# Laying the second parts of the normed tokens 448 bytes further on in SBUF, with a smaller scratch for dynamic DMAs

## The chip, the cores and the metric

The kernel is one program on one core of a Trainium2 chip. The metric is the device time of one execution in microseconds (us). Three executions of the kernel before took 2135.42, 2138.87 and 2143.49 us; the median is 2138.87 us.

## What is computed

256 tokens of width 1024 pass through two layers and a third block, all in float32. Cut to the lines that matter here, the reference is:

```python
for layer in range(2):
    x = x + mixer(x)                  # rmsnorm, x_n @ w_in, recurrence or attention, @ w_out
    x = x + peer_ffn(x)               # rmsnorm, query, top-k keys, experts
# peer_ffn, for every token t with its 8 heads and 16 chosen experts each:
#   act = gelu(<x_n[t], expert_down[idx]>);  out += g * act * expert_up[idx]
# block 2: rmsnorm, x_n @ w_in_2, pooling and dilated attention, gates, @ w_out_2, final norm
```

There are 16384 experts in a layer. The kernel does not gather the chosen ones: it multiplies the normed tokens by all of `expert_down`, masks, and multiplies by all of `expert_up`.

## The kernel before, in words

**Three matmuls for a float32 product.** Every large product is computed from parts. A float32 operand is split into a first part (rounded to float32r) and a second part (what the rounding left): `xh` and `xl` of the normed tokens, `wh` and `wl` of a weight tile. `mm3` (L431) adds three matmuls into one PSUM tile: first by first, first by second, second by first. All of them are issued in `mm` (L429), so every row of the trace has that line; they are told apart by the names of the tiles.

```python
def mm3(self, out, L, R, first, last):
    self.mm(out, L[0], R[0], start=first, stop=False)
    self.mm(out, L[0], R[1], start=False, stop=False)
    self.mm(out, L[1], R[0], start=False, stop=last)
```

`L` is the stationary operand, which a weight load (PEld) brings into the array, and `R` the moving one, which streams through it. Two kinds of product occur. In kind T the weights are stationary and the tokens move: the three matmuls are `xh,wh`, `xh,wl`, `xl,wh` of one block of 128 rows, each with 256 columns (the tokens), and the trace shows them as they run, in the order `xh,wh`, `xl,wh`, `xh,wl`. In kind N the tokens are stationary and the weights move (256, 448 or 512 columns). A group of eight such triples (24 matmuls) makes one 128x256 result.

**The tiles.** `xh` and `xl` (L388) are two tiles of 8 x 256 float32 (8192 bytes in each partition), allocated one behind the other in the pool that is opened first, and used by all five stages. `Entry.trans` (L202) and `Entry.second` (L215) fill them at the start of each stage. Split weights lie in the pool `ws` (L385, five slots of 4096 bytes for `wh`, five for `wl`), in the peer stages also in tiles `w` of their own (the query weights); `yh`, `yl`, `bh`, `bl`, `mgh`, `mgl` are the split results of block 2, multiplied by `mm3` in the same way.

**The order of the work.** The stages run one after the other: mixer 0, peer 0, mixer 1, peer 1, block 2. `Stream.run` walks a list of products and splits weights ahead of them; in a peer stage `early(e)` computes one group of 24 matmuls `ps<-x` for each of the 128 expert blocks of a layer (256 groups in all), with float16 matmuls for the masks (`oo`, `ah`) between them, and later the products with `expert_up` (`acc<-wh,W` and `acc<-wl,W`, 512 columns). ACT writes `wh` (L498), DVE `wl` (L493). SP issues the loads of weights; POOL issues a few others through its own queue, whose descriptors lie in a scratch at the start of SBUF (16384 bytes of each partition by default).

Of the kernel before, what the change touches and what calls it, by code (L numbers as in the profile page):

```python
# [8 lines left out]
F32R = mybir.dt.float32r  # L9
# [10 lines left out]
S = 256  # L20
D = 1024
KB = D // 128
# [87 lines left out]
class Lin:  # L110
# [5 lines left out]
    def __init__(self, x, W, nk, cols, cn, kind, cb, late=0, k0=0, acc=None, start=True, stop=True,  # L116
                 need=None, mid=None, of=None, pieces=None):
        self.x, self.W, self.nk, self.cn, self.kind, self.cb, self.late = x, W, nk, cn, kind, cb, late
        self.mid, self.of = mid, of
        self.pieces = pieces or range({"T": cn // 128, "N": 2, "N2": 4}[kind])  # L120
        self.k0, self.acc, self.start, self.stop, self.need = k0, acc, start, stop, need
        self.cols = cols if isinstance(cols, tuple) else (cols, cn, 1, cn)
        self.w, self.keep = [], False
        if of:
            of.keep = True
# [248 lines left out]
class Net:  # L374
    def __init__(self, ctx, tc, A):
        self.tc, self.nc, self.A, self.ctx = tc, tc.nc, A, ctx
        nc = self.nc
        P = lambda name, **k: ctx.enter_context(tc.tile_pool(name=name, **k))
        self.cp = P("consts", bufs=1)
        self.raw = P("raw", bufs=4)  # L380
        self.dram = P("dram", bufs=1, space=DRAM)
        self.n = 0
        cp = self.cp
        self.esm = P("esm", bufs=1)
        self.ws = P("ws", bufs=WS)  # L385
        self.pa = P("pa", bufs=4, space=PSUM)
        self.pb = P("pb", bufs=4, space=PSUM)
        self.xn = [cp.tile([128, KB, S], F32R, name=n) for n in ("xh", "xl")]  # L388
        self.ident = cp.tile([128, 128], F32, name="ident")
        nc.scalar.dma_start(self.ident, A["c_ident"])  # L390
        self.vec = cp.tile([128, NVEC], F32, name="vec")
        self.entry = self.brow = None
# [1523 lines left out]
```

## Time and profile before

| | |
|---|---|
| median of 3 executions | 2138.87 us (2135.42 to 2143.49) |
| the profiled execution | 2143.46 us, of which the span from first to last instruction is 2141.7 us |
| busy share of the span | PE 98%, PEld 90%, DVE 72%, ACT 53%, POOL 9% |
| granted TensorE clock, mean | 0.994 |

The profiled execution is 0.2% above the median. Matmuls are pipelined: the time given for one of them (some 280 ns for 256 columns) is from its start to its modelled end, and the next one starts while it still runs. The pace at which matmuls follow each other is read from the starts: so many matmuls between two start times. A timeline row carries its start with two decimals of a microsecond, so the pace of single matmuls is seen only over many.

### The profile page before, as it was taken

Reading aid. Unit: us, or ns where it says so; the run is one execution under the profiler, and the core shown is the slowest. Engines: PE = TensorE matmul, PEld = TensorE weight load, DVE = VectorE, ACT = ScalarE, POOL = GpSimd, SP = SyncE. Lnnn points to the kernel's source line nnn. Section 1 sums busy time; section 2 is a strip of 40 time slices with the busy share of each in tenths; the row PEclk is TensorE's granted clock in tenths of the full one; section 3 lists DMA queues with packets and bytes.
Section 4 is the critical chain, followed back from the end, with each engine's and each line's share of the span. In section 5 each row is a group of like instructions: output and inputs, shape, how many; then the busy total and the mean of one; then the engine's idle time right before and its main releaser. Section 6 shows DMA issues by size and latency. Waiting matters only on the chain.

```text
span 2141.7 us, 37623 instructions
## 1 busy us (share of the span) xinstructions
PE 2096.7 (98%) x14793; PEld 1924.8 (90%) x14793; DVE 1550.7 (72%) x2904; ACT 1124.7 (53%) x1944; POOL 198.0 (9%) x131
## 2 busy tenths in 40 slices
PE   8999999999999999998999999999999999999998
PEld 7989999999888889987799999998888899899998
DVE  7869978997666665667689789986666667644565
ACT  6345555554455454557456555555555555545443
POOL 2310210000000000012101200000000000122223
PEclk9999999999999999999999999999999999999999
DMA  7663554545666666734454645456666658475443
GB/s 247 235 228 108 180 174 153 164 150 169 195 194 191 194 197 206 251 118 138 139 187 147 198 148 159 152 163 193 193 194 195 199 193 264 154 213 147 144 145 115
DMA packets 165581, 382.19 MB, mean 178 GB/s; under 512 B 13137, under 2 KB 82444, under 8 KB 165148
## 3 DMA queue, kind: packets, MB, share of 16 engines
q1 hardware_dynamic: 160544, 364.95, 54.0%
q0 software_dynamic: 4672, 14.76, 2.0%
q8 instruction: 116, 1.90, 0.4%
q14 instruction: 61, 0.50, 0.1%
q10 hardware_dynamic: 188, 0.09, 0.0%
HBM read 376.56 MB, written 8.43 MB: 180 GB/s over the span
## 4 chain that ended last, share of the span: by engine, by line
PE 88%; DVE 8%; ACT 2%; issue 1%; DMA 1%; SPq 0%; ACTq 0%; DVEq 0%
PE acc L429 53%; PE ps L429 30%; DVE wl L493 2%; ACT wh L498 1%; PE bsc L429 1%; PE bo L429 1%; PE sc L429 0%; PE lev L429 0%; DMA wraw<-in_l_w_in_dram 0%; PE bpt L1776 0%; DVE CI L1229 0%; DVE s L1224 0%; PE ps L208 0%; ACT scr L902 0%; ACT TF L1256 0%
## 5 line engine op out<-in xcount | busy, mean ns | idle before, releaser
L493 DVE TENSOR_TENSOR wl<-raw,wh 128x1024 fp32r<-128x1024 f32 x484 | 600.1, 1250 | 134.0 <-ACT wh L498 133.2
L429 PE MATMUL acc<-wh,W 128*128 128x512 f32 x1984 | 619.6, 389 | 0.0
L429 PE MATMUL ps<-xh,wh 128*128 128x256 f32 x2048 | 582.0, 284 | 0.0
L429 PE MATMUL ps<-xh,wl 128*128 128x256 f32 x2048 | 576.0, 281 | 0.0
L429 PE MATMUL ps<-xl,wh 128*128 128x256 f32 x2048 | 575.8, 281 | 0.0
L498 ACT ACTIVATE wh<-raw 128x1024 fp32r<-128x1024 f32 x504 | 526.6, 1053 | 73.7 <-PE ps L429 55.4
L429 PEld LDWEIGHTS acc<-wh,W 128*128 128x128 f32 x1984 | 372.3, 188 | 75.8 <-DVE W L1460 0.4
L429 PEld LDWEIGHTS ps<-xl,wh 128*128 128x128 f32 x2048 | 390.7, 191 | 1.9
L429 PEld LDWEIGHTS ps<-xh,wh 128*128 128x128 f32 x2048 | 388.1, 190 | 2.0
L429 PEld LDWEIGHTS ps<-xh,wl 128*128 128x128 f32 x2048 | 388.6, 190 | 0.1
L429 PE MATMUL acc<-wl,W 128*128 128x512 f32 x992 | 386.0, 389 | 0.0
L429 PEld LDWEIGHTS acc<-wl,W 128*128 128x128 f32 x992 | 186.1, 188 | 36.9 <-DVE wl L493 0.4
L1459 ACT ACTIVATE W<-ZB 128x256 fp32r<-128x256 f32 x168 | 91.3, 543 | 176.6 <-PE acc L429 152.9
L493 DVE TENSOR_TENSOR wl<-wraw,wh 128x1024 fp32r<-128x1024 f32 (+1 forms) x110 | 144.3, 1321 | 47.9 <-ACT wh L498 47.5
L498 ACT ACTIVATE wh<-wraw 128x1024 fp32r<-128x1024 f32 (+1 forms) x140 | 144.4, 1044 | 48.3 <-PE acc L429 35.4
L1460 DVE TENSOR_TENSOR W<-ZB,W 128x256 fp32r<-128x256 f32 x168 | 89.5, 533 | 100.3 <-ACT W L1459 100.3
L429 PE MATMUL acc<-xh,wh 128*128 128x256 f32 x480 | 135.7, 283 | 0.0
L429 PE MATMUL acc<-xl,wh 128*128 128x256 f32 x480 | 132.9, 277 | 0.0
L429 PE MATMUL acc<-xh,wl 128*128 128x256 f32 x480 | 132.8, 277 | 0.0
L189 POOL TENSOR_TENSOR ZB<-X,gain 128x512 f32<-128x512 f32 x4 | 5.2, 1292 | 1276.8 <-ACT ZB L187 1276.8
L1503 ACT ACTIVATE ZB<-acc 128x352 f32<-128x352 f32 (+30 forms) x128 | 47.6, 372 | 123.2 <-PE acc L429 119.3
L429 PE MATMUL acc<-wh,xh 128*128 128x256 f32 (+2 forms) x336 | 106.7, 317 | 0.9 <-ACT scr L902 0.9
(412 smaller groups left out, 3058.8 us busy)
## 6 DMA issues: line engine op xcount, KB each, us to landing
raw<-in_l_down_t_dram SPq DMA_DIRECT2D x256, 512.0 KB, 4.3
raw<-in_l_peer_expert_up_dram SPq DMA_DIRECT2D x248, 512.0 KB, 4.3
wraw<-in_l_w_in_dram SPq DMA_DIRECT2D x36, 512.0 KB, 4.9
wraw<-in_w_in_dram SPq DMA_DIRECT2D x36, 512.0 KB, 3.9
wraw<-in_l_peer_w_query_dram SPq DMA_DIRECT2D x32, 512.0 KB, 5.1
wraw<-in_w_in_dram SPq DMA_DIRECT2D x48, 256.0 KB, 3.4
wraw<-in_l_w_out_dram SPq DMA_DIRECT2D x16, 512.0 KB, 4.4
brow<-row POOLq DMA_DIRECT2D x1, 5120.0 KB, 32.2
```

Of the source, the lines that this page charges most:

```text
L189: nc.gpsimd.tensor_tensor(y, x, self.gB[:, ns], op=OP.mult)
L429: self.nc.tensor.matmul(*a, **k)
L493: (eng or self.nc.vector).tensor_tensor(lo, r, hi.bitcast(F32), op=OP.subtract)
L498: self.nc.scalar.activation(hi, r, AF.Copy)
L1459: nc.scalar.activation(h, act, AF.Copy)
L1460: nc.vector.tensor_tensor(l, act, h.bitcast(F32), op=OP.subtract)
L1503: nc.scalar.activation(ZB[:, f - E0:, t4], pv[:, f:], AF.Copy, scale=1.0 / GSC)
```

## The change

Two edits, and no instruction is added, removed or moved: on every engine the sequence of instructions and the tiles they name are the same, only line numbers behind the first edit are two higher.

```diff
-        self.xn = [cp.tile([128, KB, S], F32R, name=n) for n in ("xh", "xl")]
+
+        self.xn = [cp.tile([128, KB * S + p], F32R, name=n)[:, q:q + KB * S].rearrange("p (k t) -> p k t", k=KB)
+                   for n, p, q in (("xh", 0, 0), ("xl", 128, 112))]
...
-    nc = _bacc.Bacc("TRN2", target_bir_lowering=False, num_devices=1)
+    nc = _bacc.Bacc("TRN2", target_bir_lowering=False, num_devices=1, dynamic_dma_scratch_size=8192)
```

The tile `xl` becomes 512 bytes longer, and the part that is used starts 448 bytes into it. The scratch of POOL's DMA queue at the start of SBUF is halved to 8192 bytes. With the longer tile alone the largest pool of the peer stage would not fit: it needs 88 kb of a partition, and 87.53 kb would be left. Everything behind `xl` therefore lies 7680 bytes lower than before (8192 less, 512 more). The byte addresses within a partition, and what is left of them after dividing by 128:

| tile | before | mod 128 | after | mod 128 |
|---|---|---|---|---|
| `xh` | 16512 | 0 | 8320 | 0 |
| `xl` | 24704 | 0 | 16960 | 64 |
| `wh`, first slot (the others 4096 apart) | 50112 | 64 | 42432 | 64 |
| `wl`, first slot (the others 4096 apart) | 70592 | 64 | 62912 | 64 |
| `w`, first of the query weights | 196672 | 64 | 188992 | 64 |
| `W`, one of two | 137152 | 64 | 129472 | 64 |
| `yh`, `yl` (block 2) | 174144, 178240 | 64 | 166464, 170560 | 64 |
| `bh`, `bl` (block 2) | 157248, 161344 | 64 | 149568, 153664 | 64 |
| `mgh`, `mgl` (block 2) | 124480, 132672 | 64 | 116800, 124992 | 64 |

The slices that one matmul reads are 512, 1024 or 2048 bytes long and start at multiples of 512 bytes within these tiles, so the remainders hold for every matmul.

## Rows read from the trace of the kernel before

**Rows 1.** The page: span, busy time of the engines, clock in 40 slices, last chain.
```profile
span 2141.7 us, 37623 instructions
...
PE 2096.7 (98%) x14793; PEld 1924.8 (90%) x14793; DVE 1550.7 (72%) x2904; ACT 1124.7 (53%) x1944; POOL 198.0 (9%) x131
...
PEclk9999999999999999999999999999999999999999
...
PE 88%; DVE 8%; ACT 2%; issue 1%; DMA 1%; SPq 0%; ACTq 0%; DVEq 0%
```

**Rows 2.** Groups by form: line, engine, tiles, shapes, count, busy us, mean ns, idle.
```profile
L429 PE MATMUL ps<-xl,wh 128*128 128x256 f32 x2048 | 575.8, 281 | 0.0
...
L429 PE MATMUL acc<-xl,wh 128*128 128x256 f32 x480 | 132.9, 277 | 0.0
...
L429 PE MATMUL acc<-wh,xl 128*128 128x256 f32 x256 | 72.2, 282 | 0.0
...
L429 PE MATMUL acc<-xl,w 128*128 128x256 f32 x192 | 53.4, 278 | 0.0
...
L429 PE MATMUL acc<-wh,mgl 128*128 128x256 f32 x64 | 18.1, 283 | 0.2 <-DVE mgl L1660 0.2
```

**Rows 3.** The chain in order of time: start us, length us, what.
```profile
282.69 25.44 PE ps L429 x216
...
1205.39 24.50 PE ps L429 x216
```

**Rows 4.** The tile xl: count, duration ns minimum/median/maximum, first and last start.
```profile
L429 PE MATMUL ps<-xl,wh x2048: 276/281/415, 156.7 to 1844.8; 128*128 128x256 f32 x187
...
L429 PE MATMUL acc<-xl,wh x480: 276/276/286, 26.4 to 2107.5; 128*128 128x256 f32 x160
```

**Rows 5.** Timeline of PE in block 2 (start, length): 192 matmuls lie between the two.
```profile
1898.44 0.28 PE L429 MATMUL acc<-xh,wh 128*128 128x256 f32 x1
...
1920.20 0.28 PE L429 MATMUL acc<-xh,wh 128*128 128x256 f32 x1
```

**Rows 6.** Timeline of PE: the first y and, 96 matmuls on, the first b.
```profile
2071.06 0.28 PE L429 MATMUL acc<-yh,wh 128*128 128x256 f32 x1
...
2082.58 0.28 PE L429 MATMUL acc<-bh,wh 128*128 128x256 f32 x1
```

**Rows 7.** Timeline of PE: a b group of 24 between two groups of x.
```profile
2090.69 0.28 PE L429 MATMUL acc<-xl,wh 128*128 128x256 f32 x1
2090.80 0.28 PE L429 MATMUL acc<-xh,wl 128*128 128x256 f32 x1
2090.91 0.28 PE L429 MATMUL acc<-bh,wh 128*128 128x256 f32 x1
2091.03 0.28 PE L429 MATMUL acc<-bl,wh 128*128 128x256 f32 x1
...
2093.76 0.28 PE L429 MATMUL acc<-xh,wh 128*128 128x256 f32 x1
```

**Rows 8.** Timeline of PE: x groups of 24 right behind y or b, and their ends.
```profile
2085.46 0.28 PE L429 MATMUL acc<-xh,wh 128*128 128x256 f32 x1
...
2088.19 0.28 PE L429 MATMUL acc<-xh,wh 128*128 128x256 f32 x1
...
2102.27 0.28 PE L429 MATMUL acc<-xh,wh 128*128 128x256 f32 x1
...
2105.01 0.28 PE L429 MATMUL acc<-xh,wh 128*128 128x256 f32 x1
```

**Rows 9.** Windows: stretch, length, busy us (count) of each engine, clock, DMA share, GB/s.
```profile
311.00:518.00 207.00, 207.00 (x1960) 203.86 (x1959) 185.45 (x309) 106.41 (x245) 0.00 (x0) 1.00 0.50 155
```

**Rows 10.** DMA queues and POOL's issues: count, KB each, median us to landing.
```profile
q0 software_dynamic: 4672, 14.76, 2.0%
...
brow<-row POOLq DMA_DIRECT2D x1, 5120.0 KB, 32.2
...
skT<-in_l_keys_t_dram POOLq DMA_DIRECT2D x2, 1024.0 KB, 10.2
```

## Prediction
> **What bounds the kernel now.** The page first: PE is busy 98% of the span, the last chain of waits is 88% PE, and the granted clock is at its full level in all 40 slices [rows 1]. So the end is set by how fast matmuls follow each other, and no wait or clock stands between them that an edit could take out. The windows say the same of the stretch that matters most, the expert products: in 207 us PE is busy 207.00 us, and DVE, the next engine, 185.45 us [rows 9]. DVE is near enough to become the bound if PE gained over 10% there, which is not in question here.
>
> The groups by form give the number of triples in kind T, the kind in which the tokens move past stationary weights: 2048 `ps`, 480 `acc` with `wh`, 192 with `w`, 2720 together [rows 2]. Their chain shows what the reader would not expect: the same 216 matmuls, with the same tiles and shapes at the same clock, take 25.44 us in one place and 24.50 us in another [rows 3], or 117.8 and 113.4 ns each. The tile `xl` shows the same two paces as durations: a single matmul of `ps` has a minimum of 276 and a median of 281 ns, of `acc` a median of 276 [rows 4]. The short pace at its cleanest lies in block 2: 192 matmuls in 1920.20 - 1898.44 = 21.76 us, 113.33 ns each, 340.0 ns a triple [rows 5]. The long pace makes 3 x 117.78 = 353.3 ns.
>
> Once in a pace, PE stays there until something interrupts it. I counted the groups of 24 by their starts in the timeline of the whole run: long are 212 of the 256 `ps` groups, 6 of the 59 whole `acc` groups and 16 of the 24 query groups. With 8 triples a group that is (212 + 6 + 16) x 8 = 1872 long triples of 2720, and the excess over an all-short run is 1872 x 13.3 ns = 25.0 us.
>
> A third pace belongs to operands that lie elsewhere. `y` moves at 64 mod 128, as its weights do: 96 matmuls take 2082.58 - 2071.06 = 11.52 us, 120.0 ns each [rows 6]. `b`, also at 64, entered from a short stretch, takes (2093.76 - 2090.91) / 24 = 118.75 ns [rows 7]. I found no group of either at 113.3. In kind N the multiplication by `mgl` at 64, and the product of `xl` at 0, have means of 283 and 282 ns: both already long [rows 2].
>
> **The change part by part.** No instruction is added, removed or moved. Three things differ.
>
> *The scratch of POOL's queue is halved.* That queue carries 4672 packets at 2.0% of the DMA engines' time [rows 10]. Its large issues are few: `brow` lands 32.2 us after issue, `skT` 10.2 us [rows 10], and their readers come far later; POOL is busy 9% [rows 1]. If descriptors had to wait for space, a landing would be late, not a matmul. Bounds: 0, and at most the three landings shown once over, 32.2 + 2 x 10.2 = 52.6 us, if each were read at once. Taken: 0, because PE waits for none of them; the cover that would have to fail is the work between issue and use.
>
> *All other tiles move down by 7680 bytes*, a multiple of 512. Their remainders, and those of `xh`, stay. In the trace the products with `w`, which starts at another multiple than `wh` but at the same remainder, have a mean of 278 ns, between the 276 and 281 of the two paces [rows 2, 4]: the remainder seems to be what matters, so 0.
>
> *`xl` goes from 0 to 64 mod 128.* It is the moving operand of one matmul in three of kind T, and the stationary one of one in three in kind N. What a mixed triple costs (two moving operands at 0, one at 64, weights at 64) no row shows, so I bound it:
> - From below: two matmuls at the short pace and one at the dearer one of `b`, 2 x 113.33 + 118.75 = 345.4 ns. All 2720 triples so: 2720 x 5.4 = 14.7 us above all-short, less the 25.0 now paid: -10.3 us.
> - From above: all three at the pace of `y`, 360.0 ns. 2720 x 20.0 - 25.0 = +29.4 us.
> - Below the lower bound: the mixture also frees the stream from the long pace and costs nothing itself, 340.0 ns: -25.0 us. No row excludes it; it is rival A.
>
> Between them I go by the nearest rows, x groups right behind `y` or `b`. Two such groups of 24 take 2088.19 - 2085.46 = 2.73 and 2105.01 - 2102.27 = 2.74 us [rows 8], against 24 x 113.33 = 2.72. So a disturbance leaves a tail of 10 to 20 ns in the matmuls after it. In the mixed triple only two matmuls at 0 follow before the next at 64; I let about 7 ns of the tail fall into them: 340 + 5.4 + 7 = about 352 ns. All 2720 triples at it: 2720 x 12 ns = 32.6, less 25.0, is +7.6 us. Every triple would then cost about what a long one costs now, and the sum differs mainly by the 848 triples that are short now (848 x 12 = 10.2 us lost, 1872 x 1.3 = 2.4 us won).
>
> In kind N `acc<-wh,xl` (256 triples) is already at 282 [rows 2]; about 3 us of excess lie there (256 x 3 x some 4 ns). It could lose as much again as `mgl` exceeds it (1 ns), or be freed: -3.4 to +1.7 us. Taken: 0.
>
> **Sum.** Scratch 0, other tiles 0, kind T +7.6, kind N 0: +7.6 us on the profiled execution of 2143.46 (span 2141.7). That execution is 0.2% above the median of 2138.87, to which I apply the difference: 2146.5 us. Own range of this case: 345.4 ns less nothing (-10.3) to a triple of 354 (2720 x 14 - 25.0 = +13.1), with kind N's +1: 2128 to 2153.
>
> **Rivals.**
> - **A: the offset keeps PE from falling into the long pace.** For it: the long pace occurs with exactly today's addresses and depends on how two streams, the moving tokens and the weight load, happen to stand to each other, since tiles, shapes and clock are the same in both [rows 3]; putting one of three reads 64 bytes elsewhere could break that lock. Against it: everything at 64 that the trace shows is dear [rows 6, 7]. All T triples short: 2138.9 - 25.0 = 2113.9 us. It decides from the point at which a mixed triple costs under 345 ns.
> - **B: the address has no effect on the pace**, the difference between x and `y` comes from something else, such as the order of stages. Then 2138.9. For it: x itself has a long pace near that of `b` (117.8 and 118.75). Against it: `y` and `b` leave the short pace at the first matmul and x returns to it within one group [rows 7, 8].
> - **C: the mixed triple locks at the pace of `y`.** 360.0 ns, +29.4 us: 2168 us, slower. Its place is the 256 `ps` groups, its price 6.7 ns a matmul; slower than now from 1872 x 13.3 / 2720 = 9.2 ns above a short triple, 349.2 ns. For it: the steady pace of `y` [rows 6] is reached where no matmul at 0 lies between; against it: two of three matmuls here are at 0.
> - **D: the smaller scratch holds POOL back**, up to the 52.6 us above, most likely some 20: 2160. Against it: the queue's 2.0% [rows 10].
>
> On B the Trainium skill has a rule ("TensorE: Matmul & The Clock Gate", Part 2, the step-by-step section): weight loads and moving operand have two independent read ports of SBUF, and loading "doesn't steal SBUF read bandwidth from the running matmul". By that rule the address of `xl` would not matter and the time would stay at 2138.9 us. The trace bears it out only in part: weight loads are busy in the same 207 us as the matmuls (203.86) without opening gaps [rows 9], but 113.3 and 117.8 ns of one shape remain unexplained by it.
>
> **How the numbers follow.** Chances: forecast 0.42, A 0.30, B 0.10, C 0.16, D 0.02. A measurement of this kernel can tell about 0.5% from no change, 10.7 us: 2128.2 to 2149.6. The forecast's case puts about 0.31 inside, 0.10 above and 0.01 below; B lies inside, A below, C and D above. Faster 0.31, same 0.41, slower 0.28. The range must hold A, which alone has 0.30, so it reaches down to 2112 (all short, and some of kind N); C and D, 0.18, may be left out, and the upper end is the forecast's own with its share of tail, 2156. As cases of both signs hold much of the chance, the likeliest one's own range is 2128 to 2153.
>
> **What would show it.** In the profile after: 216 matmuls of `ps` in the chain near 25.3 us (forecast), 24.5 (A), 25.44 in most and 24.50 in some places (B), 25.9 (C). The x groups of block 2, all short now, at 2.82 us instead of 2.72 (forecast), unchanged (A, B). The groups of `y` and `b` unchanged in any case; should they change, the address of something else matters than I think. Landings of POOL's queue as before, or D. The forecast is wrong if mixed triples settle outside 345 to 354 ns, or if they too have two paces.

## The result

The changed kernel takes 2156.99 us (median of 5 executions, 2152.13 to 2158.83) beside 2139.52 us for the kernel before (5 executions). The ratio is 1.0076, with a 95% interval from 1.0064 to 1.0088: slower by 0.76% (the medians lie 17.5 us apart), and the whole interval lies above the 0.5% that a measurement of this kernel can tell from no change. The forecast was +7.6 us. The direction that came, slower by over 0.5%, had been given a chance of 0.28, less than the 0.41 for "same".

### The profile page after: what moved, and what is told of

It reads as the page before. It is cut to its first block, busy times and chain, and to the rows that moved or that the text cites. A ratio compares the mean times of both kernels' runs of the same rounds, so it can differ in the third digit from the quotient of the medians.

```text
span 2157.1 us, 37623 instructions
## 1 busy us (share of the span) xinstructions
PE 2112.7 (98%) x14793; PEld 1938.9 (90%) x14793; DVE 1555.3 (72%) x2904; ACT 1124.6 (52%) x1944; POOL 197.4 (9%) x131
## 4 chain that ended last, share of the span: by engine, by line
PE 87%; DVE 9%; ACT 2%; issue 1%; DMA 0%; DVEq 0%; ACTq 0%
PE acc L431 54%; PE ps L431 28%; DVE wl L495 3%; ACT wh L500 1%; PE bsc L431 1%; PE bo L431 1%; PE lev L431 1%; DVE s L1226 1%; PE sc L431 0%; PE ps L208 0%; PE bpt L1778 0%; DVE eq L1309 0%; DVE CI L1231 0%; DVE eq L1312 0%; DVE eq L1305 0%
```

## The profile after

The page of the changed kernel, to be read against [rows 1]: span, busy time, chain of waits.

```profile
span 2157.1 us, 37623 instructions
...
PE 2112.7 (98%) x14793; PEld 1938.9 (90%) x14793; DVE 1555.3 (72%) x2904; ACT 1124.6 (52%) x1944; POOL 197.4 (9%) x131
...
PEclk9999999999999999999999999999999999999999
...
PE 87%; DVE 9%; ACT 2%; issue 1%; DMA 0%; DVEq 0%; ACTq 0%
```

The span grew by 15.4 us and PE's busy time by 16.0, with the same 14793 matmuls at the same clock. PE idles no more than before: 2157.1 - 2112.7 = 44.4 us against 45.0. So no wait came in; the matmuls themselves follow each other more slowly.

The landmarks of the chain in order of time (start us, length us, engine, tile, number), first in the kernel before:

```profile
509.31 269.48 PE acc L429 x1188
...
1434.26 266.41 PE acc L429 x1174
...
1866.37 56.72 PE acc L429 x462
...
2065.37 42.54 PE acc L429 x360
```

and in the changed one:

```profile
283.68 25.64 PE ps L431 x216
...
511.88 269.50 PE acc L431 x1188
...
1211.99 25.64 PE ps L431 x216
...
1443.49 266.40 PE acc L431 x1174
...
1877.02 57.73 PE acc L431 x462
...
2080.29 42.97 PE acc L431 x360
```

With the first two landmarks before in [rows 3], the shift of each start tells where the time goes: +0.99 us up to the `ps` stretch of peer 0, +1.58 through its experts to 509.31, +0.02 through the 512-column products, +6.60 - 2.59 = +4.0 up to 1205.39 (the rest of peer 0, mixer 1 and the start of peer 1), +2.6 through the experts of peer 1, +1.4 behind them, +4.3 in block 2 up to its tail, +0.5 to the end. The stretches with kind T pay, and the long stretches of 512-column products, which do not touch `xl`, take as long as before (269.50 and 266.40 us). Added up from start to start over both traces, kind T takes 15.6 us more, the 512-column products of the peer stages 1.5 more and kind N 1.0 less.

The pace itself: both `ps` stretches take 25.64 us, 118.7 ns a matmul and 356.1 ns a triple. Where before one took 25.44 and one 24.50 [rows 3], both now show the same pace. It is a mean: by the matmul that starts, the steps in `ps` (from one start to the next) are 119.7 ns (`xh,wh`), 118.8 (`xl,wh`) and 117.8 (`xh,wl`). The durations agree. Tile `xl` (count, then minimum/median/maximum ns):

```profile
L431 PE MATMUL ps<-xl,wh x2048: 277/282/415, 156.9 to 1855.5; 128*128 128x256 f32 x187
...
L431 PE MATMUL acc<-xl,wh x480: 277/283/287, 26.5 to 2122.8; 128*128 128x256 f32 x160
```

Against [rows 4] the median of `acc` went from 276 to 283. In block 2, where before 192 matmuls took 21.76 us [rows 5], the timeline of PE has

```profile
1908.93 0.28 PE L431 MATMUL acc<-xh,wh 128*128 128x256 f32 x1
...
1931.73 0.28 PE L431 MATMUL acc<-xh,wh 128*128 128x256 f32 x1
...
2086.03 0.28 PE L431 MATMUL acc<-yh,wh 128*128 128x256 f32 x1
...
2097.42 0.28 PE L431 MATMUL acc<-bh,wh 128*128 128x256 f32 x1
```

22.80 us for the same 192 (118.75 ns), and 11.39 us for the 96 of `y`, which had 11.52 [rows 6]: `y` is no dearer than `x` now, and a little cheaper than before. POOL's queue is as it was [rows 10]:

```profile
brow<-row POOLq DMA_DIRECT2D x1, 5120.0 KB, 33.0
...
skT<-in_l_keys_t_dram POOLq DMA_DIRECT2D x2, 1024.0 KB, 9.8
```

## The experiments

My theory going in was that an operand at 64 mod 128 is dear wherever the other one stands ("place"). Its rivals: what counts is how the moving operand and the weights loaded beside it stand to each other ("relation"); the scratch or the shift of everything else did it; any distance between the two parts costs. In all runs below the scratch is 8192 bytes, and r is (address of `wh` - address of the moving `xh`) modulo 512 or, once that is found to suffice, 256. The kernel before has r = 320 for both parts; in the changed kernel r is 320 for `xh` and 384 for `xl`. The query weights `w` stand elsewhere: 196672 - 50112 is 128 more than a multiple of 256, so their distance is r + 128 modulo 256.

**The scratch alone.** The changed kernel with the old line for the tiles:

```diff
-                   for n, p, q in (("xh", 0, 0), ("xl", 128, 112))]
+                   for n, p, q in (("xh", 0, 0), ("xl", 0, 0))]
```

> Scratch of 8192 bytes, xl at 0 mod 128 as before; all tiles move down by 8192 bytes. If the place of xl made the loss (my theory): ratio to before 1.000 +- 0.002, most ps stretches of 216 matmuls at 25.44 us and some at 24.50, x groups of block 2 at 2.72 us. If the smaller scratch or the shift of everything else made it: ratio 1.007 to 1.009 and stretches near 25.6 us.

Measured: 2139.41 us against 2139.66, ratio 1.000 (0.999 to 1.0009). Its chain has the short pace in both stretches of this execution:

```profile
283.99 24.50 PE ps L431 x216
...
1202.05 24.50 PE ps L431 x216
```

The scratch and the move of all tiles by a multiple of 512 cost nothing that shows; the place of `xl` is the cause. That the two stretches were long and short before, and short and short here, belongs to the scatter between the two paces: in `ps` 13% (peer 0) and 21% (peer 1) of the neighbouring starts lay at most 114 ns apart before, and 24% and 22% do here.

**Other distances for `xl` alone.** 384 bytes in place of 448 in v2, 256 in v8:

```diff
-                   for n, p, q in (("xh", 0, 0), ("xl", 128, 112))]
+                   for n, p, q in (("xh", 0, 0), ("xl", 128, 96))]
...
+                   for n, p, q in (("xh", 0, 0), ("xl", 128, 64))]
```

> Like the change, but xl starts 384 bytes into its longer tile instead of 448: 0 mod 128, 384 mod 512. If only the remainder mod 128 counts: ratio 1.000 +- 0.002, both paces as before. If any distance from a multiple of 512 between the two parts costs: ratio 1.007 to 1.009, ps stretches of 216 near 25.6 us.

> The change with 256 bytes in place of 448: xl still starts in its longer tile, scratch 8192. If the pace repeats with 256 bytes of distance, xl stands to wh as xh does, and nothing is mixed: ratio 1.000 +- 0.002, both paces, x groups of block 2 at 2.72 us. If any displacement of xl against xh costs: 1.004 to 1.008.

Measured: 384 bytes 2148.11 us, ratio 1.0044 (1.0027 to 1.006); 256 bytes 2139.39 us, ratio 0.9997 (0.9988 to 1.0007). The first fell between both expectations and refuted each: the remainder mod 128 is that of the kernel before, yet it costs over half of what the change costs. Its chain shows the long pace in both stretches,

```profile
282.46 25.45 PE ps L431 x216
...
1203.79 25.44 PE ps L431 x216
```

while 256 bytes, tried after the sweeps below had suggested a period of 256, behaves as no shift at all:

```profile
281.35 24.50 PE ps L431 x216
...
1201.91 24.50 PE ps L431 x216
```

So not every distance between the parts costs, and the remainder that counts is that mod 256.

**Place or relation.** In v3 64 bytes of padding behind the vector of constants bring the weights to 0 mod 128, where `xh` and `xl` stand unshifted; in v5 (second part of the diff, without the first) both `xh` and `xl` go to 64, where the weights stand:

```diff
-        self.vec = cp.tile([128, NVEC], F32, name="vec")
+        self.vec = cp.tile([128, NVEC + 16], F32, name="vec")[:, :NVEC]
...
-                   for n, p, q in (("xh", 0, 0), ("xl", 128, 112))]
+                   for n, p, q in (("xh", 128, 112), ("xl", 128, 112))]
```

> Scratch of 8192 and 64 bytes of padding behind the vector of constants: xh and xl stay at 0 mod 128, and all weights, y, b and mg come to 0 as well. Theory 'relation' (a matmul is dear when its moving operand and the weights loaded beside it have the same remainder): all kind T at the pace of y, 360 ns a triple, against a mean of 351: +20 to +25 us, ratio 1.009 to 1.012, and no 113.3 ns anywhere. Theory 'place' (an operand at 64 is dear wherever the other one is): all triples at 340 ns or less, y and b too, and the 512-column matmuls of expert_up below their 226.7 ns: -25 to -45 us, ratio 0.979 to 0.988. If neither counts: 1.000.

> Both xh and xl at 64 mod 128, weights at 64 as before. Theories 'relation' and 'place' both: every kind-T triple at the pace of y, 356 to 360 ns, +14 to +25 us against before, ratio 1.0065 to 1.012. If the mixture of two remainders in one triple makes the loss, and not the remainder 64 itself: as before or better, 0.99 to 1.000.

Measured: v3 2156.89 us, ratio 1.009 (1.0072 to 1.0108); v5 2158.07 us, ratio 1.0085 (1.0068 to 1.0102). v3 is the run that felled my theory: with every operand at 0 the time should have dropped by 25 us or more, and it rose by 17 us. Both runs have r = 384, and the same pace. v3:

```profile
282.75 25.63 PE ps L431 x216
...
1207.74 25.62 PE ps L431 x216
```

v5:

```profile
284.34 25.62 PE ps L431 x216
...
1211.71 25.63 PE ps L431 x216
```

The relation counts. Its size was overrated: 118.7 ns in the `ps` stretches, not the 120 of `y`. The query products bear the relation out at a second place of the weights: their mean step is 119.8 ns at distance 0 (v3, v5) and 118.7 at 128 (s1 below), close to `ps` at the same distances (119.7 and 118.9).

**The sweep over r.** `xh` and `xl` get longer tiles and an offset for each stage, the stationary `W` of the 512-column products one for each layer, so that one kernel measures several distances:

```diff
+    def xat(self, stage):
+        return [t[:, q:q + KB * S].rearrange("p (k t) -> p k t", k=KB) for t, q in zip(self.xbuf, XOFF[stage])]
...
-            xh, xl = self.xn
+            xh, xl = self.xat(f"p{l}")
...
-                        w2 = T(wk, [128, 2, S], F32R, "W")
+                        w2 = T(wk, [128, 2 * S + 128], F32R, "W")[:, WOFF[parity]:WOFF[parity] + 2 * S].rearrange("p (a t) -> p a t", a=2)
```

> Scratch 8192; xh and xl shifted together, by another amount in each stage, so that the distance r = (address of wh - address of xh) mod 512 is 192 in mixer 0, 0 in peer 0, 256 in mixer 1, 64 in peer 1, 128 in block 2 (320 in all stages before). The distance of the stationary W from the moving wh in the 512-column products is 64 in layer 0 and 128 in layer 1 (0 before). Theory 'relation mod 128' : at r = 0, 128, 256 no short pace, 356 ns a triple; at 64 and 192 both paces as before, 340 and 353; the 512-column matmuls at 64 below their 226.7 ns (by up to 6.7), at 128 unchanged. Then ps of peer 0 near 356, of peer 1 between 340 and 353, block 2 near 356. Theory 'eight places of 64 bytes' (only one or two distances are bad, r = 384 among them): 340 at most of the new distances, and the total below before by up to 20 us.

> As the sweep before it, with r = 448 in mixer 0, 128 in peer 0, 0 in mixer 1, 192 in peer 1, 256 in block 2; W against wh at 192 in layer 0 and 256 in layer 1. Relation mod 128: ps of peer 0 near 356 ns a triple, of peer 1 between 340 and 353, block 2 near 356; the 512-column matmuls below 226.7 ns in layer 0 and unchanged in layer 1. Eight places: 340 at most distances.

> As the sweeps before it, with r = 64 in mixer 0, 256 in peer 0, 192 in mixer 1, 448 in peer 1, 0 in block 2; W against wh at 320 in layer 0 and 384 in layer 1. Relation mod 128: ps of peer 0 near 356 ns a triple, of peer 1 between 340 and 353, block 2 near 356; the 512-column matmuls below 226.7 ns in layer 0 and unchanged in layer 1. Eight places: 340 at most distances.

Measured: 2167.75, 2157.81 and 2173.95 us, ratios 1.0147 (1.0123 to 1.0171), 1.009 (1.0073 to 1.0106) and 1.0168 (1.0151 to 1.0185). The chain of the first sweep, with r = 0 in peer 0 and 64 in peer 1 (`ps`), and W against `wh` at 64 and 128 (the stretches of over 1000):

```profile
281.32 25.91 PE ps L435 x216
...
511.18 277.27 PE acc L435 x1188
...
1215.88 24.50 PE ps L435 x216
...
1444.75 273.08 PE acc L435 x1174
```

the second, r = 128 and 192, W at 192 and 256:

```profile
284.73 25.63 PE ps L435 x216
...
512.74 272.07 PE acc L435 x1188
...
1210.12 25.44 PE ps L435 x216
...
1440.03 266.40 PE acc L435 x1174
```

and the third, r = 256 and 448, W at 320 and 384:

```profile
281.07 25.90 PE ps L435 x216
...
510.92 277.27 PE acc L435 x1188
...
1215.18 25.44 PE ps L435 x216
...
1445.10 274.20 PE acc L435 x1174
```

What repeats with 256 is now plain: 0 and 256 give 25.91 and 25.90, 128 and 384 give 25.63 each, 192 and 448 give 25.44 each. Of these stretches only those at 64 and 320 have the 24.50. The rule of mod 128 was right for 0, 128 and 256 and wrong for 192 and 448: the long pace is there, but hardly a short one (counted in the trace, 2% of the neighbouring starts of `ps` lie at most 114 ns apart, against 33% at r = 64). The query products, which stand at 192 in the kernel before, say otherwise: 34% of their steps are short there. So 192 has both paces too, and r alone does not tell how often the short one occurs. The 512-column products went the other way than expected: 269.48 and 266.41 us at 0 are the best, 64 costs 7.8 us and 128 6.7 (384 in the third sweep 7.8), and the losses of the first sweep are 14.5 of the 28 us by which the first sweep's kernel is slower.

**Between the multiples of 64.** Only the numbers in the two tables of offsets change.

> After the sweeps the pace of kind T repeats with 256 bytes of distance r: 119.7 ns at 0 and 256, both paces (33% of the matmuls short) at 64, 118.8 at 128 and 384, 117.7 and never short at 192 and 448; the 512-column matmuls have 226.7 to 227.3 at 0 and 256 and 229 to 233 elsewhere. Here r is 32 in peer 0, 96 in peer 1, 64 in all of block 2, 192 in mixer 1 (kind N), and 320 in mixer 0; W against wh at 32 in layer 0 and 224 in layer 1. If the reads go in pieces of 64 bytes: r = 32 and 96 behave like one of their neighbours (119.7 or 118.8, or both paces). If the distance counts byte by byte: means between the neighbours, 117 to 119. If some finer distance is free of the loss: 113.3 in a peer stage, 10 us less for that stage. Block 2 at 64 as at 320: near 114.1 ns with 0.8 of the matmuls short.

> As the run before it, with r = 48 in peer 0, 80 in peer 1, 72 in block 2, 64 in mixer 0, 448 in mixer 1; W against wh at 16 in layer 0 and 240 in layer 1. Pieces of 64 bytes: 48 and 80 like one of their neighbours; byte by byte: both near the 116.4 of 64, a little above; a free distance: 113.3. The 512-column matmuls at 16 and 240 near the 226.7 of 0, or below if a small distance frees them (220).

Measured: 2165.15 and 2162.79 us, ratios 1.0129 (1.0112 to 1.0146) and 1.0116 (1.009 to 1.0141). The tail of block 2 is shown too. r = 32 and 96, block 2 at 64:

```profile
282.41 25.55 PE ps L435 x216
...
1213.77 25.35 PE ps L435 x216
...
2086.39 42.54 PE acc L435 x360
```

r = 48 and 80, block 2 at 72:

```profile
284.33 25.75 PE ps L435 x216
...
1208.81 25.76 PE ps L435 x216
...
2081.76 43.17 PE acc L435 x360
```

None of the three ideas holds quite. Over its whole stage 96 lies between its neighbours (118.5 ns), and so does 32 (118.3). But 16 bytes above 64 the short pace is gone (119.3 ns, none of the steps short), and 16 bytes below it 9% of the steps are short, though the stretch of the chain is a long one (119.2 ns). Block 2 at r = 64 keeps its tail of 360 matmuls at 42.54 us, as at 320; at 72 that takes 43.17. Between its `x` matmuls that is 114.1 and 119.9 ns: the short pace exists at r = 64 and is gone 8 bytes above it. The 512-column products took 228.0 and 228.5 ns at 16 and 240, above the 226.7 of 0 and not below, and 233.4 and 233.3 at 32 and 224; at those two distances they make most of the loss of the first of these runs.

In one table: a `ps` stretch of 216 in us and by 216 in ns, then the whole stage, as the mean of the neighbouring `ps` starts up to 135 ns apart and the share of them that is short (at most 114 ns):

| r mod 256 | stretch, us | stretch, ns | stage, ns | short |
|---|---|---|---|---|
| 0 | 25.90, 25.91 | 119.9 | 119.7 | 1% |
| 32 | 25.55 | 118.3 | 118.3 | 0% |
| 48 | 25.75 | 119.2 | 118.6 | 9% |
| 64 | 24.50 or 25.44 | 113.4 or 117.8 | 116.3 to 117.2 | 13 to 33% |
| 80 | 25.76 | 119.3 | 119.3 | 0% |
| 96 | 25.35 | 117.4 | 118.5 | 1% |
| 128 | 25.62, 25.63 | 118.7 | 118.9 | 0% |
| 192 | 25.44 | 117.8 | 117.7, 117.8 | 2% |
| `xh` 64, `xl` 128 (the change) | 25.64 | 118.7 | 118.8 | 4% |
| `xh` 64, `xl` 192 (v2) | 25.44, 25.45 | 117.8 | 117.8 | 2 to 4% |

**A better place.** In v2 kind N of block 2 had become short (113.2 and 114.0 ns between starts, where before it had 117.8), and there the stationary parts, `xh` and `xl`, stood at 192 and 64. So the same was tried for kind T: the second part of the weights 128 bytes further on, the moving parts together. In s6 this holds for `ps`, with `wh` and `wl` at 64 and 192 in peer 0 and, by moving `xh` and `xl` 128 bytes there, at 192 and 64 in peer 1; in s7 they are at 64 and 192 in both, and in the queries too (the last part of the diff, in s7 alone):

```diff
+WLQ = 32
...
-        hi, lo = places or (pool.tile([128, 1024], F32R, name=self.uid(t), tag=t)[:, :n] for t in ("wh", "wl"))
+        if places:
+            hi, lo = places
+        else:
+            hi = pool.tile([128, 1024], F32R, name=self.uid("wh"), tag="wh")[:, :n]
+            lo = pool.tile([128, 1024 + (64 if pool is self.ws else 0)], F32R, name=self.uid("wl"), tag="wl")[:, q:q + n]
...
-                         for x in self.split_weights(self.ws, down_raw.pop(e), eng=eng)]
+                         for x in self.split_weights(self.ws, down_raw.pop(e), eng=eng, q=WLQ)]
...
-                    hl, r = T(wp, [128, 2, 1024], F32R, "w"), units[u]
+                    hl, r = T(wp, [128, 2048 + 64], F32R, "w"), units[u]
+                    hl = [hl[:, 32:1056], hl[:, 1088:2112]]
```

> A search for a better place, from one finding: in the run with xl 384 bytes further (v2), kind N of block 2, whose stationary operands xh and xl stood at r = 192 and 64, ran at 113.2 to 114.0 ns with 0.97 of the matmuls short, while kind T, whose moving operands were mixed in this way, lost its short pace. Here the stationary operands of ps are mixed instead: wl of expert_down lies 128 bytes further than wh (modulo 256), so that wh and wl stand at r = 64 and 192 in peer 0, and at 192 and 64 in peer 1 (there xh and xl are both shifted by 128 bytes); all else as before. If mixing the stationary operand frees the short pace: ps near 340 ns a triple in one or both peer stages, 10 us less for each, down to 2117 to 2121 us, ratio 0.990. If any mixture costs, as in the change: 353 to 356, ratio 1.002 to 1.005.

> xh and xl as before; the second part of the weights at r = 192 and the first at 64, in the ps groups of both peer stages and in the queries (in the run before, peer 0 had it so: 84% of its matmuls short, 114.2 ns; peer 1, the other way round, 51% and 115.9). Scratch 8192. Expected: ps at 114.2 ns in both stages, 1024 triples x 3 x 1.7 = 5 us less than that run, and about 1 us from the queries: 2124 us, ratio 0.992 to 0.994. If peer 1 stays at 115.9: 2130, ratio 0.996.

Measured: s6 2131.19 us, ratio 0.996 (0.9946 to 0.9974); s7 2125.39 us against 2139.85, ratio 0.9938 (0.9924 to 0.9951), faster than both kernels. The chain of s6, peer 0 and peer 1,

```profile
279.61 24.52 PE ps L436 x216
...
1190.98 25.68 PE ps L436 x216
```

of s7,

```profile
280.41 24.54 PE ps L432 x216
...
1190.23 24.52 PE ps L432 x216
```

and its groups by form; the mean of the first of them was 281 ns before [rows 2]:

```profile
L432 PE MATMUL ps<-xl,wh 128*128 128x256 f32 x2048 | 567.6, 277 | 0.0
L432 PE MATMUL ps<-xh,wl 128*128 128x256 f32 x2048 | 567.6, 277 | 1.3 <-DVE wl L496 1.3
```

Counted by neighbouring starts, some 85% of the `ps` steps of s7 are short, where 13% (peer 0) and 21% (peer 1) were before. In s6 peer 0 has 85% and peer 1, with the two distances the other way round, 52% (116.0 ns on average, though the stretch of its chain is a long one). So in `ps` 64 for the first part and 192 for the second is the better order, and the reverse still beats both at 64. In kind N the order 192, 64 held 97% (block 2 of v2); why the order counts in one and not in the other is open.

## Why the prediction came out as it did

**What bounds the kernel** held: PE, its pace, no wait and no clock. The place where the change would act held too: the loss is in kind T, 15.6 us of a growth of 15.4, with small terms of both signs beside it.

**The step that failed in size** is the price of a mixed triple: "I let about 7 ns of the tail fall into them: 340 + 5.4 + 7 = about 352 ns". It costs 356.1 ns. In place of 2720 x 12 ns the term is 2720 x 16.1 = 43.8 us, and less the 25.0 that the long pace already cost the sum is +18.8, not +7.6. The idea behind it, two matmuls at the short pace and one disturbed, is not what happens: all three steps of the triple are long, 117.8 to 119.7 ns, with the mean of a stream that is wholly at r = 128. The bounds of 345.4 and 360.0 held it; the forecast's own range ended at 354. Kind T grew by 15.6 us in the two traces, 3.2 less than 18.8. Of these, 2.4 lie in interruptions of `ps`: starts more than 135 ns apart, 133 of them with 37.8 us before, 103 with 31.9 after; over 118 ns each that is an excess of 22.1 and 19.7 us. Whether the change did this is not shown: v8, at the pace of the kernel before, has 103 with 31.5 us too. Kind N, which I set to 0, gained 1.0 us; in block 2 its steps went from 117.8 to 115.6 ns. Its upper bound of +1.7 us does not follow from the 1 ns given for it (256 x 3 x 1 ns is 0.8 us); only the +1 at the upper end of the forecast's own range rests on it.

**The step that failed in kind** is the reason given for it, "everything at 64 that the trace shows is dear", read as the remainder of one tile mod 128. Neither place, 0 or 64 mod 128, is dear in itself (v3, v5); what counts is the distance between the moving operand and the weights, mod 256. `y`, `b` and `mgl` are dear because they stand at 128 mod 256 from their weights, not because they stand at 64. By its shift `xl` went from 64 to that same distance. The conclusion for `xl` came out right by luck of the addresses: for moving operands the rows had shown 64 mod 128 only in that relation. The query weights, taken as proof that the remainder mod 128 is what matters, stood at 192 where `wh` stands at 64: at the two distances the long paces are alike (117.8 ns), which hid the difference. The other zero, for tiles that move by a multiple of 512, was right (v1).

**The rivals.** A (the offset frees the stream) is refuted for this change, but not foolish: moving another second part, that of the weights, frees most of the stream in s7. Its condition, a mixed triple under 345 ns, was the right one to name. B (no effect) is refuted by v1 beside the change: same scratch, 1.000 against 1.0076. The Trainium skill's rule that was weighed there ("TensorE: Matmul & The Clock Gate", Part 2, step by step: two read ports, and loading weights takes no bandwidth from the running matmul) leaves no room for the distance of the two operands; here, with the same instructions, that distance alone moves the pace from 113.4 to 119.9 ns, and the measurement decides. C (the pace of `y`, 360 ns) came nearer than the forecast did, 3.9 ns off where I was 4.1: about a draw, with the truth between. D is refuted by v1, and by landings that stayed at 33.0 and 9.8 us.

**The chances.** 0.28 for slower, of which C had 0.16 and the forecast's upper tail 0.10, was too little; the 0.30 for A rested on the argument that any displacement might break a lock, and I had no row for it. The outer range, 2112 to 2156, holds 2138.87 x 1.0076 = 2155.1; the median of the changed kernel's own runs is 1 us above it. With a growth of more than twice the forecast, that it came so near the edge and not beyond it is luck. Of the signs named, the chain near 25.3 us came out at 25.64, the `x` groups of block 2 at 24 x 118.75 = 2.85 us instead of 2.82, and "`y` and `b` unchanged" was wrong for `y`, by 1.35 ns a matmul.

**What stays open.** That weight loads and moving reads meet somewhere that repeats with 256 bytes fits the long paces of all runs, but it is a guess: no run separates the weight load from the matmul. Why at r = 64 or 192 a stream can be in either of two paces, what decides which, and why the order 64, 192 of the stationary parts in `ps` holds the short one, is not explained. Nor is `y`, whose distance of 128 did not change while its pace went from 120.0 to 118.65 ns. The share of short steps varies from one execution to the next at the same addresses mod 256 (`ps` of peer 0: 13% before, 24% in v1, 21% in v8), and each share here is from one trace, so small differences of shares between distances mean little.

## What to carry to other kernels

When PE is busy all the time and the same matmul shows two paces at the same clock, look at the addresses: sort the steps between starts by (weights - moving operand) mod 256 and move tiles by 64 or 128 bytes to the best class, operand pair by operand pair, since it is a relation and helping one pair can hurt another. Measure each class before you shift anything; a few stages with different offsets in one kernel do that in one run. And do not price a mixture as the sum of its parts. Moving parts that alternated between 64 and 128 ran at the pace of the dearer distance throughout (118.8 ns); between 192 and 0, in the queries of the changed kernel, at 118.8, between the two. Stationary parts that alternated between 192 and 128 ran faster than at either distance alone (kind N of block 2: 115.6 ns after the change, against 117.8 at 192 before and 118.7 at 128 in v3).

## What was not expected of the hardware

- The time between 256-column float32r matmuls, each with its own weight load, depends on the distance of the two operands in a partition: 113.4 to 119.9 ns. Distances that differ by 256 bytes gave the same long pace wherever two were tried (0 and 256, 64 and 320, 128 and 384, 192 and 448). For the 512-column ones (1188 in a stretch) it is 269.48 / 1188 = 226.8 ns at 0 and 277.27 / 1188 = 233.4 at 64: the distance that is best for one is among the worst for the other.
- 8 bytes are enough to lose the short pace (block 2, r = 72: 43.17 us for the tail of 360 matmuls, against 42.54 at 64).
- Two moving parts at 64 and 192 lose the short pace (v2: 25.45 and 25.44 us for a `ps` stretch); two stationary parts at 64 and 192 hold it (s7: 24.54 and 24.52 us).
